# Where the split pieces of the down weights stand in the instruction order of a fused encoder layer

## The chip, the cores and the metric

The kernel runs on one core of a Trainium2 chip. A core has a matrix engine (TensorE, PE in the profile), a vector engine (VectorE, DVE), an activation engine (ScalarE, ACT), a general engine (GpSimd, POOL) and a queue engine (SyncE, SP) that issues all DMAs here. Each engine takes its instructions strictly in the order in which they stand in its queue. The metric is the device time of one launch in microseconds, median of three runs.

## The reference, cut to what matters

One encoder layer over 2048 tokens of width 1024, in float32: a normalised input projection, two groups of attention heads, an output projection with a residual, and a feed-forward block of inner width 4096. The change lies in the last one and in what leads to it:

```python
x = x + jnp.concatenate([o_mla, o_diff], axis=-1) @ w_out[layer]

h = _rmsnorm(x, mlp_norm_w[layer])
x = x + jnp.square(jax.nn.relu(h @ w_up[layer])) @ w_down[layer]
```

## The kernel before, in words

**Precision and products.** Each float32 operand is held as two float16 parts, `h` (high) and `l` (low), so that one product is three matmuls (lines 134 to 136). `split` makes the two parts: a copy on ACT (line 129 or, with a scale, line 130) and a subtraction on DVE (the same lines). Both halves of the feed-forward block use a seven-product scheme in place of eight block products, so weights and activations are first combined by additions on POOL and then split into seven pieces.

**Stages.** Projections and attention fill the first 1410 us. The output projection `out_proj` follows to about 1625 us, in 16 rounds `i`, one for each tile of 128 tokens. It also transposes the normalised tokens (`out_back`) and combines them in pairs (`combine_rows`). Tokens of the first column half (`c = 0`) stay in SBUF in seven tiles of the pool "L". Those of the second half (`c = 1`) are stored piece by piece to DRAM, `hcD`, 28 stores, and read back as `hT[1, i]`, fourteen tiles of the pool "W", 56 loads.

**Up steps.** 32 steps `n` follow, one for each pair of weight columns `p` and token half `c`. A step (`up_step`) has seven products named X1, Z5, X6, Y2, X7, Z3, X4 after their PSUM bank and number, each of 12 matmuls. X1 and X6, X7, X4 add up in the same bank, so each of them must wait until the last result has been read: X1 is copied by line 1300, Z5 by 1306, X6 by 1309 (ACT); Y2, X7 and Z3 are added by 1312, 1316 and 1321 (DVE). Line 1300 writes the tile `ca` of the pool "X4". X4 of a step is issued after X1 of the next one (`tail`). Then `up_rest` combines the results (POOL, 1350 to 1359), splits them (ACT 1346, DVE 1347) and stores them to DRAM as `uD`.

**Down steps.** Eight groups `g` of two weight pairs; in each, four double steps `i`, each for two token tiles. A double step (`down_steps`) runs the same seven names over both tiles, 14 products of six matmuls. X1, Z5 and X6 are copied out by `keep` (ACT, line 1453, into the pool "N2"); Y2, X7, Z3 and X4 are added into float32 sums by `add` (DVE, line 1457, and for three of the four names POOL, line 1459, which frees the "N2" tile).

**The pieces of the down weights.** `down_weights(g)` is a generator of 14 pieces: seven results for each of the two weight pairs, in the order in which the products of the next group use them. A piece is at most one addition on POOL (1400, 1402, 1404, 1406) and one `split` (line 130 on ACT and DVE). Its scale comes from `down_max` (maxima on DVE, 1220), `down_front` and `down_scale` (through 1376). Small pieces of work such as these are queued in `behind_products`; `tick(n)` takes the next `n` of them, so the ticks say where in the program they stand.

**What sets the order.** The matmuls are chained by hand (`ordered`). All else is placed by a list scheduler at build time: it puts on each engine what its timing model says is ready, and it gives a tile a buffer when its pool has a free one. A piece can therefore stand earlier in the engine's queue than where the program emitted it. `set_fence(ins)` remembers the last instruction of an engine, and `behind(ins)` forbids that an instruction stands ahead of it; neither adds a wait on the chip. The pools used here have 7 ("L"), 22 ("W"), 8 ("P"), 3 ("X4") and 6 ("N2") buffers.

Of the kernel before, what the change touches and what calls it, by code (L numbers as in the profile page):

```python
# [50 lines left out]
def encoder_layer(ctx: ExitStack, tc: tile.TileContext, a, out, stop=None):  # L51
# [192 lines left out]
    oD = [dram(f"oD{i}", [P, 2 * H, P]) for i in range(NT)]  # L244
    x2D = [dram(f"x2D{i}", [P, D]) for i in range(NT)]

    hcD = [dram(f"hcD{i}", [P, 7, 2, 512], F16) for i in range(4)]

    uD = [dram(f"uD{g}", [8, P, GP, 7, 2, P], F16) for g in range(NPAIR // GP)]

# [823 lines left out]
    def out_back(t):  # L1074
        y = ys.pop(t)
        if t == 0:
            for i in range(7):
                b = sb("L", [P, 2, 4, 512], F16)
                hT[0, i] = b[:, 0], b[:, 1]
        st = stage[t] = sb("P", [P, 2, 512])  # L1080
        for hf in range(2):
            pt = ps()
            for k in range(4):
                c = 4 * hf + k
                ordered(nc.tensor.transpose(pt[:, k * P : (k + 1) * P], y[:, c * P : (c + 1) * P], ident))
            for k in range(4):
                c = W_ML + 4 * hf + k
                act(st[:, hf, k * P : k * P + P], pt[:, k * P : k * P + P], AF.Copy, scale=wvec[:, c : c + 1])
        if t < 8:
            return  # L1090
        tq = t % 4

        def put(i, x):
            if t < 12:
                split(hT[0, i][0][:, tq], hT[0, i][1][:, tq], x)
            else:
                o = sb("N2", [P, 2, 512], F16)
                split(o[:, 0], o[:, 1], x)
                dma(hcD[tq][:, i].rearrange("p l c -> p (l c)"), o.rearrange("p l c -> p (l c)"))

        behind_products.append(combine_rows(stage.pop(t - 8), stage.pop(t), put))

# [2 lines left out]
    def out_proj():  # L1105
# [12 lines left out]
        for i, t in enumerate(order):  # L1118
            if i + 2 < NT:
                ot[i + 2] = out_scale(*out_load(order[i + 2]))  # L1120
            hfs = (0, 1)[i == 0 :]
            out_mid(t, 0, *mix, hfs)
            tick(2)
            nxt = list(out_front(ot.pop(i + 1))) if i + 1 < NT else [None]
            if i >= 2:
                out_back(order[i - 2])
            tick(1)
            out_mid(t, 1, *mix, hfs)
            mix = nxt[-1]
            if i == 1:  # L1130
                ml_setup()
            out_norm(t)
            tick(2)
            if i == 3:
                down_load(0, "W")
            if i == 4:
                behind_products.append(down_max(0))
            for p, j in enumerate((4, 7, 13)):
                if i == j:
                    up_load(p, "W" if p < 2 else "X4")  # L1140
                if i == j + 1:
                    behind_products.append(up_stat(p))
                if i == j + 3 and p < 2:
                    up_scale(p)
                    behind_products.append(up_weights(p))
            yield
# [69 lines left out]
    def down_max(g):  # L1216

        m = dmx[g] = small("dmx", [P, 2 * GP])
        for i, r in enumerate(rawd[g]):
            V.tensor_reduce(m[:, i : i + 1], r.rearrange("p h c -> p (h c)"), AX, ALU.max, apply_absolute_value=True)  # L1220
            yield
        if g == 0:
            rawd.pop(g)
# [52 lines left out]
    def up_step(n, c, p, hook, per):  # L1276
# [15 lines left out]

        u11, u21, u12, u22 = ca[:, 0], ca[:, 1], cb[:, 0], cb[:, 1]

        def square(x):
            act(x, x, AF.Relu)
            act(x, x, AF.Square)

        prod(X, 1, True)
        act(u11, X, AF.Copy, scale=US)  # L1300
# [2 lines left out]
        tails.clear()  # L1303
        tick(per)
        prod(Z, 5, True)
        act(u22, Z, AF.Copy, scale=US)
        tick(per)
        prod(X, 6, False)
        act(u12, X, AF.Copy, scale=US)  # L1309
        tick(per)  # L1310
        prod(Y, 2, True)
        V.scalar_tensor_tensor(u11, Y, US, u11, ALU.mult, ALU.add)
        square(u11)
        tick(per)
        prod(X, 7, False)
        V.scalar_tensor_tensor(u22, X, US, u22, ALU.mult, ALU.add)
        square(u22)
        tick(per)
        hook()
        prod(Z, 3, False)  # L1320
        V.scalar_tensor_tensor(u12, Z, US, u12, ALU.mult, ALU.add)
        V.scalar_tensor_tensor(u12, u12, 0.0, u12, ALU.max, ALU.mult)
        tick(per)

        def tail():
# [56 lines left out]

    def down_weights(g):

        t = [sb("L", [P, 2, GP, 2, 512], F16) for _ in range(3)] + [sb("W", [P, 1, GP, 2, 512], F16)]
        w = wdn[g] = [t[s // 2][:, s % 2] for s in SLOT]
        r = rawd.pop(g)
        sums = [sb("X4", [P, 2, 512]) for _ in range(GP)]

        def put(q, i, x):  # L1390
            c = dsc[g][:, q : q + 1]
            split(w[i][:, q, 0], w[i][:, q, 1], x, c)

        for j in range(7):
            for q in range(GP):
                ra, rb_ = r[2 * q : 2 * q + 2]
                b11, b12, b21, b22 = ra[:, 0], ra[:, 1], rb_[:, 0], rb_[:, 1]
                t1, t2 = sums[q][:, 0], sums[q][:, 1]
                if j == 0:
                    G.tensor_tensor(t1, b12, b11, ALU.subtract)  # L1400
                elif j == 1:
                    G.tensor_tensor(t2, b22, t1, ALU.subtract)
                elif j == 2:
                    G.tensor_tensor(b12, b22, b12, ALU.subtract)
                elif j == 4:
                    G.tensor_tensor(b21, b21, t2, ALU.subtract)
                put(q, *((0, b11), (3, t1), (4, t2), (1, b21), (5, b12), (2, b22), (6, b21))[j])
                yield

# [23 lines left out]
    TURN = ({"X": 0, "Z": 2, "Y": 4}, {"X": 6, "Z": 4, "Y": 2})  # L1433

    def down_steps(g, n, taus, hook):
        part = {}
        bk = {(t, b): bank[TURN[n % 2][b] + i] for i, t in enumerate(taus) for b in "XYZ"}
        w, lam = wdn[g], dsc[g][:, GP + 2 : GP + 3]

# [10 lines left out]
        def keep(t, name, to):  # L1450

            part[t, to] = x = sb("N2", [P, 512])
            act(x, bk[t, name], AF.Copy, scale=lam)  # L1453

        def add(t, name, to):
            x = accs[t][to]
            V.scalar_tensor_tensor(x, bk[t, name], lam, x, ALU.mult, ALU.add)  # L1457
            if (t, to) in part:
                G.tensor_tensor(x, x, part.pop((t, to)), ALU.add)  # L1459

        for name, n, first, then, to in (
            ("X", 1, True, keep, 0),
# [9 lines left out]
            for t in taus:  # L1472
                prod(t, name, n, first)
                then(t, name, to)
                tick(1)

    steps = [(p, c) for c in range(2) for p in range(4)]
    steps += [(p, c) for p in range(4, NPAIR - 2) for c in range(2)]
# [5 lines left out]
    for n, (p, c) in enumerate(steps):  # L1484
# [2 lines left out]
            drain(made[n])  # L1487
        if n == 1:
            drain(made["tokens"])
            for i in range(7):  # L1490
                b = hT[1, i] = [sb("W", [P, 4, 512], F16) for _ in range(2)]
                for l in range(2):
                    for tq in range(4):
                        dma(b[l][:, tq], hcD[tq][:, i, l])
        if n and nxt is not None:
            made[n + 1] = up_weights(nxt)
            behind_products.insert(0, made[n + 1])
# [2 lines left out]
        if n == last_step - 1:  # L1500
            down_load(0, "L")
        if n == last_step:
            made["down"] = down_weights(0)
            behind_products.append(made["down"])
            down_u(0, (0, 1), "L")

        def hook():
# [8 lines left out]
                    behind_products.append(made[nxt3, "stat"])  # L1516
            if n == 3:
                down_scale(0)

        up_step(n, c, p, hook, 4 if n in (0, last_step) else 2)  # L1520
        if nxt2 is not None and nxt2 not in scaled:
            if (nxt2, "stat") in made:
                drain(made[nxt2, "stat"])
# [99 lines left out]
```

## Time and profile before

| | |
|---|---|
| median of 3 runs | 2865.11 us (2864.14 to 2866.52) |
| profiled execution | 2862.0 us, its span 2860.2 us |
| mean granted TensorE clock | 0.987 |
| busy, share of the span | PE 94%, DVE 75%, ACT 61%, POOL 60% |
| up steps | about 1625 to 2247 us |
| down steps | about 2247 to 2857 us |

The span runs from the first instruction to the last; the 1.8 us beside it are start and end. A busy PE is not a PE at its peak. A full-speed product of 512 columns starts 0.216 us after the one before, and an idle PE shows as a larger step between two starts.

### The profile page before, as it was taken

The page shows a single profiled execution, that of the slowest core. Times are in us where ns is not written, and L with a number is a line of the kernel's source. Part 1 is how long each engine was busy: PE and PEld are TensorE (multiplying, and loading weights), DVE is VectorE, ACT ScalarE, POOL GpSimd, SP SyncE. Part 2 cuts the span into 40 slices and gives each one's busy share as a digit, 9 for nine tenths or more (in the row PEclk, how much of TensorE's full clock was granted, in tenths as well). Part 3 has the DMA queues.
Part 4 walks back from the last instruction along what each step waited for, and adds up shares of the span by engine and source line. Part 5 has one row for each costly group of instructions (what it writes and reads, how often), then busy time and mean ns, then how long its engine had stood idle before and what let it go on. Part 6 is the DMA issues. An engine that isn't in the chain of part 4 may idle for free. (4 is left out here: it accounts for less than half of the span.)

```text
span 2860.2 us, 47994 instructions
## 1 busy us (share of the span) xinstructions
PE 2686.4 (94%) x16904; PEld 1574.4 (55%) x16904; DVE 2140.0 (75%) x4292; ACT 1735.5 (61%) x3814; POOL 1715.3 (60%) x1404
## 2 busy tenths in 40 slices
PE   7999998999999999889899988999999899999999
PEld 6878885666656666556555434444444344444444
DVE  8767778999998999889868777777776655555543
ACT  6545556888888888778757656666666433333332
POOL 5434334888888888778724355444444755565544
PEclk9999999999999999999999999999999999999999
DMA  5445557998999999899844753444444643333334
GB/s 194 123 116 133 136 131 186 199 204 184 203 207 200 195 203 204 189 197 188 207 165 146 241 175 107 133 133 133 133 146 158 234 151 133 133 123 116 133 103 169
DMA packets 994514, 469.35 MB, mean 164 GB/s; under 512 B 776128, under 2 KB 943040, under 8 KB 994272
## 3 DMA queue, kind: packets, MB, share of 16 engines
q1 hardware_dynamic: 994272, 466.29, 62.7%
q8 instruction: 132, 2.16, 0.3%
q14 instruction: 110, 0.90, 0.1%
HBM read 168.39 MB, written 132.12 MB: 105 GB/s over the span
## 5 line engine op out<-in xcount | busy, mean ns | idle before, releaser
L762 ACT ACTIVATE P<-D,nm,one 128x512 f32<-128x512 f32 x768 | 587.2, 774 | 132.0 <-DVE nm L756 70.8
L735 PE MATMUL D<-W,X 128*128 128x512 f16 x2304 | 573.0, 384 | 61.6 <-ACT P L762 58.7
L819 POOL TENSOR_TENSOR L<-P,L 128x1024 f16<-128x1024 f32 x256 | 553.9, 2172 | 32.4 <-ACT L L813 21.8
L750 DVE TENSOR_REDUCE nmx<-D 128x1 f32<-128x512 f32 (+3 forms) x768 | 450.8, 619 | 38.3 <-PE D L735 32.1
L836 PE MATMUL O<-W,L 128*128 128x128 f16 x2048 | 363.0, 220 | 16.3 <-DMA L<-L 9.1
L1459 POOL TENSOR_TENSOR W<-W,N 128x512 f32<-128x512 f32 x192 | 242.6, 1273 | 222.6 <-DVE W L1457 220.0
L735 PEld LDWEIGHTS <-X 128*128 128x128 f16 x2304 | 214.2, 99 | 282.7 <-issue 94.3
L837 PE MATMUL O<-W,L 128*128 128x128 f16 x2048 | 362.8, 220 | 1.1 <-DVE W L130 1.1
L838 PE MATMUL O<-W,L 128*128 128x128 f16 x2048 | 363.0, 220 | 0.0
L1457 DVE SCALAR_TENSOR_TENSOR W<-D,dsc,W 128x512 f32<-128x512 f32 x224 | 166.3, 747 | 255.8 <-PE D L136 255.8
L134 PE MATMUL D<-W,W 128*128 128x512 f16 (+2 forms) x822 | 313.6, 382 | 24.1 <-ACT P L1309 11.4
L135 PE MATMUL D<-W,W 128*128 128x512 f16 (+2 forms) x822 | 313.3, 381 | 3.2 <-DVE W L130 3.2
L136 PE MATMUL D<-W,W 128*128 128x512 f16 (+2 forms) x822 | 312.9, 381 | 0.6 <-DVE W L130 0.5
L140 POOL TENSOR_SCALAR L<-P 128x1024 f16<-128x1024 f32 x128 | 223.1, 1743 | 138.7 <-ACT P L762 138.7
L134 PE MATMUL D<-L,W 128*128 128x512 f16 (+1 forms) x644 | 249.5, 387 | 18.0 <-ACT X L1300 12.1
L134 PE MATMUL D<-L,P 128*128 128x512 f16 x648 | 247.1, 381 | 14.5 <-ACT N L1453 14.2
L135 PE MATMUL D<-L,W 128*128 128x512 f16 (+1 forms) x644 | 247.4, 384 | 0.0
L136 PE MATMUL D<-L,W 128*128 128x512 f16 (+1 forms) x644 | 247.3, 384 | 0.0
L135 PE MATMUL D<-L,P 128*128 128x512 f16 x648 | 246.9, 381 | 0.0
L136 PE MATMUL D<-L,P 128*128 128x512 f16 x648 | 246.8, 381 | 0.0
L836 PEld LDWEIGHTS <-L 128*128 128x128 f16 x2048 | 201.2, 98 | 53.0 <-DMA L<-L 15.7
L837 PEld LDWEIGHTS <-L 128*128 128x128 f16 x2048 | 201.2, 98 | 46.2 <-issue 12.8
(421 smaller groups left out, 5729.5 us busy)
## 6 DMA issues: line engine op xcount, KB each, us to landing
P<-uD SPq DMA_DIRECT2D x124, 448.0 KB, 4.9
uD<-P SPq DMA_DIRECT2D x96, 512.0 KB, 3.2
P<-in_w_up_dram SPq DMA_DIRECT2D x34, 512.0 KB, 4.7
W<-in_w_down_dram SPq DMA_DIRECT2D x32, 512.0 KB, 4.1
X<-in_x_dram SPq DMA_DIRECT2D x17, 512.0 KB, 3.6
vD<-N SPq DMA_DIRECT2D x32, 256.0 KB, 2.6
qA<-N SPq DMA_DIRECT2D x32, 256.0 KB, 2.6
oD<-N SPq DMA_DIRECT2D x128, 64.0 KB, 2.6
```

Source lines behind the costliest of these rows:

```text
L134: mm(o, ah, bh, start=first, stop=False, skip_group_check=more),
L135: mm(o, ah, bl, start=False, stop=False, skip_group_check=more),
L136: mm(o, al, bh, start=False, stop=last, skip_group_check=more),
L140: return G.tensor_scalar(o, i, sc, 0.0, ALU.mult, ALU.add)
L735: ordered(mm(s, st, mv[:, kc], start=j == 0, stop=j == len(self.passes) - 1))
L750: ordered(V.tensor_reduce(self.nmx[:, self.n : self.n + 1], s[:, c0 * P : c1 * P], AX, ALU.max))
L762: last_exp[:] = [act(o, self.ch[c], AF.Exp, bias=self.nm, scale=self.sg, accum_out=self.sm[:, c : c + 1])]
L819: ordered(G.tensor_tensor(hl[:, 1], self.soft[d].p[hf], hl[:, 0], ALU.subtract))
L836: ordered(mm(od, hT_, v[:, 0], start=kb == 0, stop=False))
L837: ordered(mm(od, hT_, v[:, 1], start=False, stop=False))
L838: ordered(mm(od, lT_, v[:, 0], start=False, stop=kb == NT - 1))
L1459: G.tensor_tensor(x, x, part.pop((t, to)), ALU.add)
```

## The change

- `down_steps`: each `keep` and `add` sets the fence of its engine. In the double steps `i` = 2 and 3 a tick follows only the first of the two tiles' products, so 7 pieces fall in each of the two instead of all 14 in `i` = 2.
- `down_weights`: all its instructions stand behind the fences. The tile of the seventh result is taken from "W" only when it is made. For the first group the sums lie in "P" and no longer in "X4".
- `down_max`: the maxima stand behind the fence.
- In the last two up steps the copies, squares and additions set fences. The first group's pieces are queued from the hook of the last but one up step, no longer from the start of the last; the last up step takes three pieces at each tick and no longer four.
- `up_load` of pair 2 takes its raw weights from "W" and no longer from "X4".
- `hcD` is laid out by result and not by tile of tokens: 28 stores as before, each in rows of 1 KB instead of 2 KB, and 14 loads in rows of 4 KB instead of 56 in rows of 1 KB. A load now needs the stores of all four tiles. The loads are emitted in two up steps (five results at `n` = 1, two at `n` = 2).

```diff
-    hcD = [dram(f"hcD{i}", [P, 7, 2, 512], F16) for i in range(4)]
+    hcD = [dram(f"hcD{i}", [2, P, 4, 512], F16) for i in range(7)]
...
-                dma(hcD[tq][:, i].rearrange("p l c -> p (l c)"), o.rearrange("p l c -> p (l c)"))
+                dma(hcD[i][:, :, tq].rearrange("l p c -> p l c"), o)
...
-                    up_load(p, "W" if p < 2 else "X4")
+                    up_load(p, "W")
...
# down_max
-            V.tensor_reduce(m[:, i : i + 1], r..., AX, ALU.max, apply_absolute_value=True)
+            behind(V.tensor_reduce(m[:, i : i + 1], r..., AX, ALU.max, apply_absolute_value=True))
...
# up_step
+        mark = set_fence if n >= last_step - 1 else lambda *ins: None
         def square(x):
             act(x, x, AF.Relu)
-            act(x, x, AF.Square)
+            mark(act(x, x, AF.Square))
...
-        act(u22, Z, AF.Copy, scale=US)
+        mark(act(u22, Z, AF.Copy, scale=US))
...      (the same for u12 after X6, and for the additions after Y2, X7 and Z3)
# down_weights
-        t = [sb("L", ...) for _ in range(3)] + [sb("W", [P, 1, GP, 2, 512], F16)]
-        w = wdn[g] = [t[s // 2][:, s % 2] for s in SLOT]
+        t = [sb("L", ...) for _ in range(3)]
+        w = wdn[g] = [t[s // 2][:, s % 2] for s in SLOT[:6]]
-        sums = [sb("X4", [P, 2, 512]) for _ in range(GP)]
+        sums = [sb("X4" if g else "P", [P, 2, 512]) for _ in range(GP)]
         def put(q, i, x):
-            split(w[i][:, q, 0], w[i][:, q, 1], x, c)
+            behind(*split(w[i][:, q, 0], w[i][:, q, 1], x, c))
         for j in range(7):
+            if j == 6:
+                w.append(sb("W", [P, GP, 2, 512], F16))
...
-                    G.tensor_tensor(t1, b12, b11, ALU.subtract)
+                    behind(G.tensor_tensor(t1, b12, b11, ALU.subtract))
...      (the same for the other three additions)
# down_steps
-        part = {}
+        part, rare = {}, n >= 2
...
-            act(x, bk[t, name], AF.Copy, scale=lam)
+            set_fence(act(x, bk[t, name], AF.Copy, scale=lam))
...
-            V.scalar_tensor_tensor(x, bk[t, name], lam, x, ALU.mult, ALU.add)
+            set_fence(V.scalar_tensor_tensor(x, bk[t, name], lam, x, ALU.mult, ALU.add))
             if (t, to) in part:
-                G.tensor_tensor(x, x, part.pop((t, to)), ALU.add)
+                set_fence(G.tensor_tensor(x, x, part.pop((t, to)), ALU.add))
...
-                tick(1)
+                if not rare or t == taus[0]:
+                    tick(1)
# the loop over up steps
-            for i in range(7):
+        if n in (1, 2):
+            for i in ((0, 3, 4, 1, 5), (2, 6))[n - 1]:
                 b = hT[1, i] = [sb("W", [P, 4, 512], F16) for _ in range(2)]
                 for l in range(2):
-                    for tq in range(4):
-                        dma(b[l][:, tq], hcD[tq][:, i, l])
+                    dma(b[l].rearrange("p t c -> p (t c)"), hcD[i][l].rearrange("p t c -> p (t c)"))
...
         if n == last_step:
-            made["down"] = down_weights(0)
-            behind_products.append(made["down"])
             down_u(0, (0, 1), "L")
         def hook():
...
+            if n == last_step - 1:
+                made["down"] = down_weights(0)
+                behind_products.append(made["down"])
-        up_step(n, c, p, hook, 4 if n in (0, last_step) else 2)
+        up_step(n, c, p, hook, {0: 4, last_step: 3}.get(n, 2))
```

More of the change, by code (lines that the diff above doesn't have):

```diff
@@ L1219, in down_max @@
         for i, r in enumerate(rawd[g]):
-            V.tensor_reduce(m[:, i : i + 1], r.rearrange("p h c -> p (h c)"), AX, ALU.max, apply_absolute_value=True)
+            behind(V.tensor_reduce(m[:, i : i + 1], r.rearrange("p h c -> p (h c)"), AX, ALU.max, apply_absolute_value=True))
             yield
@@ L1305, in up_step @@
         prod(Z, 5, True)
-        act(u22, Z, AF.Copy, scale=US)
+        mark(act(u22, Z, AF.Copy, scale=US))
         tick(per)
         prod(X, 6, False)
-        act(u12, X, AF.Copy, scale=US)
+        mark(act(u12, X, AF.Copy, scale=US))
         tick(per)
         prod(Y, 2, True)
-        V.scalar_tensor_tensor(u11, Y, US, u11, ALU.mult, ALU.add)
+        mark(V.scalar_tensor_tensor(u11, Y, US, u11, ALU.mult, ALU.add))
         square(u11)
@@ L1315, in up_step @@
         prod(X, 7, False)
-        V.scalar_tensor_tensor(u22, X, US, u22, ALU.mult, ALU.add)
+        mark(V.scalar_tensor_tensor(u22, X, US, u22, ALU.mult, ALU.add))
         square(u22)
@@ L1321, in up_step @@
         V.scalar_tensor_tensor(u12, Z, US, u12, ALU.mult, ALU.add)
-        V.scalar_tensor_tensor(u12, u12, 0.0, u12, ALU.max, ALU.mult)
+        mark(V.scalar_tensor_tensor(u12, u12, 0.0, u12, ALU.max, ALU.mult))
         tick(per)
@@ L1383, in down_weights @@
     def down_weights(g):
-        t = [sb("L", [P, 2, GP, 2, 512], F16) for _ in range(3)] + [sb("W", [P, 1, GP, 2, 512], F16)]
-        w = wdn[g] = [t[s // 2][:, s % 2] for s in SLOT]
+        t = [sb("L", [P, 2, GP, 2, 512], F16) for _ in range(3)]
+        w = wdn[g] = [t[s // 2][:, s % 2] for s in SLOT[:6]]
         r = rawd.pop(g)
-        sums = [sb("X4", [P, 2, 512]) for _ in range(GP)]
+        sums = [sb("X4" if g else "P", [P, 2, 512]) for _ in range(GP)]
         def put(q, i, x):
             c = dsc[g][:, q : q + 1]
-            split(w[i][:, q, 0], w[i][:, q, 1], x, c)
+            behind(*split(w[i][:, q, 0], w[i][:, q, 1], x, c))
         for j in range(7):
+            if j == 6:
+                w.append(sb("W", [P, GP, 2, 512], F16))
             for q in range(GP):
@@ L1399, in down_weights @@
                 if j == 0:
-                    G.tensor_tensor(t1, b12, b11, ALU.subtract)
+                    behind(G.tensor_tensor(t1, b12, b11, ALU.subtract))
                 elif j == 1:
-                    G.tensor_tensor(t2, b22, t1, ALU.subtract)
+                    behind(G.tensor_tensor(t2, b22, t1, ALU.subtract))
                 elif j == 2:
-                    G.tensor_tensor(b12, b22, b12, ALU.subtract)
+                    behind(G.tensor_tensor(b12, b22, b12, ALU.subtract))
                 elif j == 4:
-                    G.tensor_tensor(b21, b21, t2, ALU.subtract)
+                    behind(G.tensor_tensor(b21, b21, t2, ALU.subtract))
                 put(q, *((0, b11), (3, t1), (4, t2), (1, b21), (5, b12), (2, b22), (6, b21))[j])
```

## Prediction

> **What bounds the kernel now.** I read the first page, then the waits of PE in four windows, then the timelines of single engines around the longest of these waits.
>
> ```profile
> span 2860.2 us, 47994 instructions
> PE 2686.4 (94%) x16904; PEld 1574.4 (55%) x16904; DVE 2140.0 (75%) x4292; ACT 1735.5 (61%) x3814; POOL 1715.3 (60%) x1404
> ...
> PE D L134 <- ACT X L1300: 12.1, 2, 11.3
> PE D L134 <- ACT P L1309: 1.2, 1, 1.2
> ...
> PE D L134 <- ACT P L1309: 15.0, 8, 2.8
> ...
> PE D L134 <- DVE P L1316: 5.3, 1, 5.3
> PE D L134 <- ACT N L1453: 2.6, 1, 2.6
> PE D L134 <- ACT P L1309: 0.9, 1, 0.9
> ...
> PE D L134 <- ACT N L1453: 14.2, 7, 2.4
> PE D L134 <- DVE W L1457: 3.3, 7, 0.7
> ```
>
> The matrix engine bounds the kernel. The wait rows (idle in total, times, longest) are of the windows 1625 to 1668, 1668 to 2218, 2218 to 2266 and 2266 to 2860 us. The number of matmuls doesn't change, so the change can only give back these waits, 55 us in all, or add new ones. Idle understates a stall: a full-speed product follows the last after 0.216 us but is shown as busy for 0.38, so each stall costs 0.16 us more, and after some of them PE runs at half speed for a while (below). The 15.0 us in the second window lie in steps that the change doesn't touch.
>
> **Term 1, the down groups.** This is one of the seven groups that prepare the next; the others look the same.
>
> ```profile
> 2436.45 1.33 ACT L130 ACTIVATE L<-W,dsc 128x512 f16<-128x512 f32 x2 [8.68 <-DVE dsc L1376]
> 2437.69 2.54 ACT L130 ACTIVATE L<-X,dsc 128x512 f16<-128x512 f32 x4
> 2440.14 3.77 ACT L130 ACTIVATE L<-W,dsc 128x512 f16<-128x512 f32 x6
> 2443.82 2.38 ACT L1453 ACTIVATE N<-D,dsc 128x512 f32<-128x512 f32 x4
> ...
> 2444.53 0.38 PE L134 MATMUL D<-L,P 128*128 128x512 f16 x1 [1.78 <-ACT N L1453]
> ...
> 2439.53 2.73 DVE L130 SCALAR_TENSOR_TENSOR L<-X,dsc,L 128x512 f16<-128x512 f32 x4
> ...
> 2451.97 1.21 DVE L1220 TENSOR_REDUCE dmx<-W 128x1 f32<-128x1024 f32 x1
> 2453.10 1.39 DVE L1457 SCALAR_TENSOR_TENSOR W<-D,dsc,W 128x512 f32<-128x512 f32 x2
> ...
> 2455.98 0.38 PE L134 MATMUL D<-W,P 128*128 128x512 f16 x1 [0.66 <-DVE W L1457]
> ...
> 2596.98 0.38 PE L134 MATMUL D<-L,P 128*128 128x512 f16 x1 [2.35 <-ACT N L1453]
> 2598.14 0.63 PE L135 MATMUL D<-L,P 128*128 128x512 f16 x1
> 2600.70 0.50 PE L135 MATMUL D<-L,P 128*128 128x512 f16 x1
> ```
>
> As soon as the scale is there, ACT runs twelve splits in a row (7.4 us), and the four copies that free X wait behind them: PE loses 1.78 + 0.16 us. The DVE maxima of a later group stand ahead of the additions and cost two shorter stalls. Between the stalls at 2444.53 and 2596.98 lie two groups: 152.5 us, 76.2 each. A double step has 14 x 6 = 84 matmuls; four of them with two small ones are 338 x 0.216 = 72.9 us. So a group loses 3.3 us, and seven groups 23 to 24: 17.5 us of idle, 14 x 0.16, twice about 1.7 us of half speed after a stall of 2.35 (from the row at 2598.14 to that at 2600.70 six steps take 2.56 us, 0.43 each), and about 1 us of gaps too short for the list.
>
> After the change no split stands ahead of the `keep` or `add` before it, and one piece comes to two products, 2.59 us. In the copy phase ACT has two copies of 0.60 and a split of 0.64 there (rows: 2.38 and 2.54 for four): 1.8 us, no queue. In the adding phase DVE has two additions of 0.70 and a subtraction of 0.68 (1.39 for two, 2.73 for four): 2.1 us. The tied maxima go to the start of the second double step, when no additions are due; the scale is taken at the same point as before. The last piece comes with the last product of the group, but it feeds the seventh product of the next one, 12 products or 15.5 us later; pieces are made in the order of use. The raw tiles come free some 18 us later, so the four loads of a later group move to the first double step, 18 us before their maxima. "W" still suffices: 16 sums, 4 raw tiles, 2 seventh pieces are its 22.
>
> ```profile
> 2448.79 3.26 DVE L130 SCALAR_TENSOR_TENSOR W<-W,dsc,W 128x512 f16<-128x512 f32 x2
> ...
> 2443.00 5.59 POOL L1406 TENSOR_TENSOR W<-W,X 128x512 f32<-128x512 f32 x2 [5.38 <-DVE L L130]
> 2451.46 1.71 POOL L1404 TENSOR_TENSOR W<-W,W 128x512 f32<-128x512 f32 x1
> 2453.98 1.27 POOL L1459 TENSOR_TENSOR W<-W,N 128x512 f32<-128x512 f32 x1 [0.80 <-DVE W L1457]
> ```
>
> What hides the pieces is slack: a copy or addition has three products (3.9 us) before its bank is written again. If POOL runs beside it, a subtraction takes up to 1.63 us (3.26 for two) and the pair of products 3.0 instead of 2.59. Over three pairs that is a lag of 1.3 us, still inside 3.9 less the 0.7 of the addition. I take 22.5 of the 24 us, with ends 10 (a lag comes back as 1 us of stall in each of 14 double steps) and 24.
>
> [...]
>
> [...]
>
> **Term 2, the step after the output projection.**
>
> ```profile
> 1660.66 0.58 PE L134 MATMUL D<-L,W 128*128 128x512 f16 x1 [11.27 <-ACT X L1300]
> ...
> 1659.13 0.68 DVE L1347 TENSOR_TENSOR N<-X,N 128x512 f16<-128x512 f32 x1
> ...
> 1660.03 0.57 ACT L1300 ACTIVATE X<-D 128x512 f32<-128x512 f32 x1
> ...
> 1644.00:1662.00 18.00, 6.74 (x29) 2.85 (x28) 17.97 (x18) 11.58 (x16) 11.22 (x8) 0.72 0.91 288
> ```
>
> Line 1300 of step 1 started 0.2 us after line 1347 had read the last of step 0's `ca`. The pool "X4" has three buffers, and the raw weights of pair 2 held two. With "W" for these, `ca` has a buffer at once and the stall of 11.4 us goes, and with it the half speed after it, about 2 us by the 1.7 above: 13.4 together. What is late next: the window row (us; busy of PE, PEld, DVE, ACT, POOL; clock; DMA share and GB/s) shows DVE full and the DMA at 0.91 in this stretch. Up to there a stall covered them. Moreover, the loads of `hcD` now wait for the last stores and come after 1640 us, where before they began at 1606 (row below).
>
> ```profile
> L116 SPq DMA_DIRECT2D W<-hcD x56: 319/430/2193, 1606.1 to 1655.8; - x56
> W<-x2D SPq DMA_DIRECT2D x16, 512.0 KB, 9.0
> 2244.82 8.28 SPq L116 DMA_DIRECT2D W<-x2D  x8
> ```
>
> SP gains: 56 issues of 0.43 us (24 us of its queue) become 14. The bytes stay, 14 tiles of 512 KB; eight loads of this form and size were let go in 8.28 us, about 1.2 us each when back to back, so 14 take some 17 us: 1640 to 1665 us, with uD stores and raw weights between them. They are first needed in step 4: step 1 began three products before the stall (1649 - 7.8), and three steps of 18.1 later it is 1696. Stores of `uD` behind them may land 5 us later and hold "P" buffers. I take 4 us of new stall (ends 0 and 11), and 1 us back from line 1309 in step 0, which stood behind splits of the tokens: 10.4 us. The 28 stores have twice the rows, 256 KB each as before; at 28 spread over 70 us I cost them at nothing, bounded by the 4 us.
>
> **Term 3, the end of the up steps.**
>
> ```profile
> 2221.25 1.27 POOL L1400 TENSOR_TENSOR X<-L 128x512 f32<-128x512 f32 x1
> 2232.88 2.13 POOL L1400 TENSOR_TENSOR X<-L 128x512 f32<-128x512 f32 x1 [1.88 <-issue]
> ...
> 2232.67 1.21 DVE L1347 TENSOR_TENSOR P<-X,P 128x1024 f16<-128x1024 f32 x1
> 2240.50 1.75 DVE L130 SCALAR_TENSOR_TENSOR L<-X,dsc,L 128x512 f16<-128x512 f32 x1
> 2242.17 0.68 DVE L1316 SCALAR_TENSOR_TENSOR P<-D,P 128x512 f32<-128x512 f32 x1
> ...
> 2242.90 0.59 PE L134 MATMUL D<-W,W 128*128 128x512 f16 x1 [5.26 <-DVE P L1316]
> ...
> 2260.69 0.69 ACT L1453 ACTIVATE N<-D,dsc 128x512 f32<-128x512 f32 x1 [1.82 <-POOL W L1459]
> ```
>
> The first sums waited for "X4" buffers until 2221 and 2233, so the pieces crowded the last 20 us, each subtraction at up to 1.75 us. Here 5.26 + 2.63 + 0.9 us of idle, three times 0.16 and about 1.5 us of half speed make 10.8. After the change the sums have "P" buffers, and the POOL additions, which no fence of these steps holds, can run 15 us earlier. But the splits that ran ahead in step 30 are tied too: 14 subtractions of 0.68 (9.5 us), those of `up_rest` (3 x 1.21 + 0.68) and four additions of 0.68 are 16.5 us of DVE in a step of 84 x 0.216 = 18.1. It fits with little to spare; three pieces between two products can hold line 1316 up to 2 us too long, and the "N2" wait at 2260.69 can partly stay. The two "L" tiles of the first activations are now taken after the three of the pieces, some microseconds later than now and some 30 before their use: nothing. I take 3 us of new stalls (ends 0 and 11): 7.8 us gained.
>
> **The sum.** 22.5 + 10.4 + 7.8 = 40.7 us from the profiled execution of 2862.0 us, which stands 3.1 us under the median of 2865.1. Prediction 2824 us.
>
> **Rivals.**
> A. Part of the stalls come back. For: POOL in double steps 2 and 3 has 12 additions of line 1459 and 8 of the pieces, 20 x 1.27 = 25.4 us; its row of 5.59 for two beside DVE's splits shows that these can hold it up, and if each of the 14 does so for its whole 0.68, 9.5 more make 34.9 of 36.3 us. DVE is full in step 1. Against: the blocks rarely meet in full. If 1.5 us stay in each group and terms 2 and 3 give half: 13.5 + 9.1 = 23 us, 2842.
> B. The fences only forbid earlier places; the scheduler puts the pieces later, and they crowd at the end of the group. Then the first products of the next one wait as now: term 1 goes, terms 2 and 3 stay at 18, 2847; if the same holds in step 31, 2855. Against: a ready piece was always taken at once.
> C. No change: term 1 by B, and DVE and DMA in step 1 hand back the 10 us of term 2: within 6 us of 2865.
> D. Slower: POOL becomes the bound of double steps 2 and 3. At a mean of 2.3 us per addition, as POOL's row of 2.13 or 5.59 for two suggest, 20 take 46 us for 36.3, 10 over; through "N2" the copies and so PE wait for it. Seven times 10, less 41, is 29 us slower, 2894. It decides from (36.3 + 41/7)/20 = 2.1 us on. Against: those rows lie beside unbroken DVE work, which the change breaks up; line 1459 alone shows 1.27.
>
> **How the numbers follow.** Forecast 0.62 (2806 to 2835), A and B together 0.23 (2835 to 2856), C 0.06, D 0.09. A measurement here can tell about 0.2%, 5.7 us. Faster 0.85, same 0.06, slower 0.09. Lower end: all three terms in full, 24 + 14.4 + 10.8 = 49, and a further 8 of the 15 us of line 1309 by a luckier order: 2808, put at 2807. Upper end: A and most of B, 2850. The likeliest case alone spans 2810 to 2835.
>
> **What would show it.** Term 1: splits of line 130 single between copies of line 1453, no PE wait on line 1453 in double step 2, groups of 73 us. Term 2: no PE wait on line 1300; loads of `hcD` after 1640 us. Term 3: line 1400 near 2200, the wait on line 1316 under 2 us. Wrong would be: PE waits on line 1457 or on "N2" in both double steps, POOL without gaps there, or a first matmul of step 4 that waits for `hcD`.

## The result and the profile after

The changed kernel takes 2832.81 us (median of four runs; 2828.2 to 2836.23) against 2865.12 us (2864.14 to 2866.52) before: a ratio of 0.9882 with a 95% interval of 0.9867 to 0.9896, 32.3 us less. The forecast was 2824. The profiled execution of the changed kernel took 2831.03 us. Lines below 1300 keep their numbers; 1300 is now 1302, 1309 is 1311, 1316 is 1318, 1346 and 1347 are 1348 and 1349, 1453 is 1458, 1457 is 1462 and 1459 is 1464.

The first page, its two lines on the span and the engines:

```profile
span 2829.2 us, 47941 instructions
...
PE 2684.3 (95%) x16904; PEld 1574.7 (56%) x16904; DVE 2169.4 (77%) x4292; ACT 1738.0 (61%) x3814; POOL 1713.2 (61%) x1404
```

The busy time of PE is the same as before to 2 us, so the gain is time in which PE no longer stands. The waits of PE after the change (idle in total, times, longest), in the windows 1625 to 1668, 1668 to 1900, 2218 to 2266 and 2266 to 2829 us:

```profile
PE D L134 <- ACT X L1302: 0.8, 1, 0.8
...
PE D L134 <- ACT P L1311: 8.1, 6, 2.3
PE D L136 <- DVE W L130: 7.3, 5, 4.2
PE D L134 <- ACT W L130: 3.1, 2, 2.9
...
PE D L134 <- ACT N L1458: 2.0, 1, 2.0
...
PE D L134 <- ACT N L1458: 0.4, 1, 0.4
```

The kernel before had, in the second of these windows:

```profile
PE D L134 <- ACT P L1309: 12.8, 6, 2.8
PE D L136 <- DVE W L130: 0.5, 1, 0.5
```

The last window, seven down groups, has lost its 17.5 us of idle but for 0.4. In the third the 5.3 us on the addition is gone. In the first the 12.1 us on line 1300 is down to 0.8. But in the second, in steps whose matrix work the change doesn't touch, 10.4 us of waits for splits of line 130 stand where 0.5 us stood.

A stall costs more than its idle, as the prediction worked out (0.16 us more each, from 0.38 and 0.216 us a product, and half speed after some), so I also summed by how much each matmul starts later than 0.216 us after the start before it. Figures called lost below are such sums over the records of a trace, in us:

| window | before | after |
|---|---|---|
| 1620 to 1668, step 1 | 17.0 | 3.8 |
| 1668 to 1900 | 14.6 | 25.0 |
| 1900 to 2215 | 2.8 | 3.2 |
| 2215 to 2266 | 10.8 | 2.5 |
| 2266 to the end | 24.4 | 0.6 |

That is 34.5 us less, and the profiled executions differ by 31.0. The rest lies in the attention stage, which the change does not touch: matmul number 10,349, at its end, starts at 1412.2 us in the trace of before and at 1416.0 in that of after, and between 1411.5 and 1420.1 in all traces of this case. Some differences below are therefore also given as one trace of each kernel shows them from that matmul to the last.

How a down group looks now, ACT and then DVE, in order of time, from the changed kernel:

```profile
2426.66 0.69 ACT L1458 ACTIVATE N<-D,dsc 128x512 f32<-128x512 f32 x1 [11.18 <-PE D L136]
2427.25 0.71 ACT L130 ACTIVATE L<-W,dsc 128x512 f16<-128x512 f32 x1
2427.97 0.69 ACT L1458 ACTIVATE N<-D,dsc 128x512 f32<-128x512 f32 x1
...
2435.05 0.74 DVE L130 SCALAR_TENSOR_TENSOR L<-X,dsc,L 128x512 f16<-128x512 f32 x1
2435.71 0.74 DVE L1462 SCALAR_TENSOR_TENSOR W<-D,dsc,W 128x512 f32<-128x512 f32 x1
...
2442.84 1.66 DVE L130 SCALAR_TENSOR_TENSOR L<-W,dsc,L 128x512 f16<-128x512 f32 x1
```

One split stands between two copies, where twelve stood in a row, and one subtraction between two additions; that of 2442.84, with two additions of POOL beside it (line 1464, 2442.69 to 2445.62 us), takes 1.66 us, and still no product waits for an addition.

### The profile page after: what moved, and what is told of

Read it like the earlier page. It is cut to its first block, busy times and chain, and to the rows that moved or that the text cites. A ratio compares the mean times of both kernels' runs of the same rounds, so it can differ in the third digit from the quotient of the medians.

```text
span 2829.2 us, 47941 instructions
## 1 busy us (share of the span) xinstructions
PE 2684.3 (95%) x16904; PEld 1574.7 (56%) x16904; DVE 2169.4 (77%) x4292; ACT 1738.0 (61%) x3814; POOL 1713.2 (61%) x1404
## 4 chain that ended last, share of the span: by engine, by line
PE 36%; DVE 7%; ACT 2%; POOL 2%; DMA 2%; issue 2%; POOLq 0%; SPq 0%; ACTq 0%; DVEq 0%
PE D L134 10%; PE D L136 10%; PE D L135 10%; DVE W L130 2%; DVE P L1349 1%; PE O L134 1%; PE O L136 1%; PE O L135 1%; DMA uD<-P 1%; DVE N L1171 1%; ACT P L1348 1%; DMA P<-in_w_up_dram 1%; POOL P L1352 0%; POOL P L1353 0%; DVE P L1324 0%
## 5 line engine op out<-in xcount | busy, mean ns | idle before, releaser
L1464 POOL TENSOR_TENSOR W<-W,N 128x512 f32<-128x512 f32 x192 | 262.4, 1381 | 235.9 <-DVE W L1462 224.8
L1458 ACT ACTIVATE N<-D,dsc 128x512 f32<-128x512 f32 x160 | 109.8, 687 | 209.4 <-PE D L136 204.4
L836 PEld LDWEIGHTS <-L 128*128 128x128 f16 x2048 | 201.4, 98 | 51.6 <-DMA L<-L 14.1
```

What stands on the lines that cost most here:

```text
L836: ordered(mm(od, hT_, v[:, 0], start=kb == 0, stop=False))
L1464: set_fence(G.tensor_tensor(x, x, part.pop((t, to)), ALU.add))
```

## Where the time came back

The reading goes backwards from the first long new stall, with PE, then ACT and POOL of the changed kernel:

```profile
1691.45 0.39 PE L134 MATMUL D<-L,W 128*128 128x512 f16 x1 [2.85 <-ACT W L130]
...
1693.90 0.63 PE L136 MATMUL D<-L,W 128*128 128x512 f16 x1
...
1685.25 1.06 ACT L1348 ACTIVATE P<-X 128x1024 f16<-128x1024 f32 x1 [4.52 <-DMA uD<-P]
1690.68 0.72 ACT L130 ACTIVATE W<-N,rb_b 128x512 f16<-128x512 f32 x1 [1.04 <-POOL N L1193]
...
1687.71 1.26 POOL L1361 TENSOR_TENSOR X<-X,P 128x512 f32<-128x512 f32 x1 [12.40 <-DVE P L1349]
1688.94 1.71 POOL L1193 TENSOR_TENSOR N<-P 128x512 f32<-128x512 f32 x1
```

PE waits for a split of the next pair's weights; that split waits for POOL's sum on line 1193; the sum stands in POOL's order behind line 1361, for which POOL idles 12.40 us; line 1361 needs the last read of a hidden block, lines 1348 and 1349; and line 1348 waits 4.52 us until a store of `uD` lets go of a "P" buffer. After the stall PE runs at half speed (the row of 0.63 us; such products start 0.43 us apart, and the granted clock is 0.50 from 1693.4 to 1696.6 us): with it and two short waits for the next splits, 6.5 us are lost from 1688 to 1699 us.

Why is the store late? SP of the changed kernel, and then the answers for the tile `hcD` and, from 1650 to 1692 us, for the tile `uD` (in the `hcD` row: ns of an issue, shortest, median and longest, then the us at which the first and the last start):

```profile
1654.37 3.60 SPq L116 DMA_DIRECT2D W<-hcD  x7
1658.06 0.38 SPq L116 DMA_DIRECT2D uD<-P  x1
...
1671.93 3.29 SPq L116 DMA_DIRECT2D W<-hcD  x4
1676.42 2.78 SPq L116 DMA_DIRECT2D uD<-P  x2
...
L116 SPq DMA_DIRECT2D W<-hcD x14: 333/441/1238, 1637.4 to 1674.3; - x14
...
DMA to landing us min/median/max: 4.0/7.6/12.1
```

Each load reads the rows of all four tiles of tokens, so it can't be let go before the last tile's store. After three single ones they come in bursts, seven (3.5 MB) and then four, with `uD` stores right behind. A store lands up to 12.1 us after its issue, that of 1658.06; the first of the two from 1676.42, behind the four loads, lands at 1685.2, and then line 1348 starts. Over the whole kernel the median to landing is 3.2:

```profile
uD<-P SPq DMA_DIRECT2D x96, 512.0 KB, 3.2
```

These rows show the order and the times, not that the loads ahead make a store late; loads_by_tile and last_loads_later below test that.

A second place, 1754 to 1768 us, loses 8.4 us in the same trace, 4.2 of them in one wait for a split: a raw tile of `w_up` arrives late, and the square of line 1168, which waits for it, stands ahead of two splits on ACT:

```profile
1753.14 1.06 ACT L1168 ACTIVATE N<-P 128x1024 bf16<-128x1024 f32 x1 [3.07 <-DMA P<-in_w_up_dram]
```

## The experiments

The kernels ran in three sets of four, each set on one chip beside the kernel before. The median of before was 2866.7 us in the first set (up to after_pair2_in_x4), 2865.81 in the second (no_fence_in_groups, all_ticks_in_third, old_layout_of_tokens, squares_behind_splits) and 2866.55 in the third.

### Each part alone

The theory is that three parts act in separate windows and that their gains add up, with the second reduced by new stalls; the rival is that they need each other.

**groups_alone**: of the change, only the fences in `down_steps`, `behind` in `down_max` and `down_weights`, the seventh piece's own "W" tile and the ticks over two double steps.

```diff
-            split(w[i][:, q, 0], w[i][:, q, 1], x, c)
+            behind(*split(w[i][:, q, 0], w[i][:, q, 1], x, c))
...
-            act(x, bk[t, name], AF.Copy, scale=lam)
+            set_fence(act(x, bk[t, name], AF.Copy, scale=lam))
...
-                tick(1)
+                if not rare or t == taus[0]:
+                    tick(1)
```

> The kernel before with the edits of the down groups alone: fences in the double steps, pieces and maxima behind them, a tick after only the first tile in the last two double steps; tokens, pool of pair 2 and the first group as before. Theory (the term of the groups is worth what the changed kernel's trace shows there, 24 us, and stands by itself): 23 to 25 us faster than before, groups of 73 us. Rival (the groups' gain is partly due to the earlier stages, which then set other places for the scheduler): under 18 us.

Measured 2839.7 us (2837.77 to 2843.17), 0.9908 [0.9887, 0.9929]: 27.0 us less. Waits of PE in the windows from 1625, from 2215 and from 2266 us:

```profile
PE D L134 <- ACT X L1300: 12.1, 2, 11.3
...
PE D L134 <- DVE P L1316: 5.3, 1, 5.3
...
PE D L134 <- ACT N L1455: 1.1, 2, 0.7
```

The 17.5 us of the groups are down to 1.1, and the long stalls of the other two terms stand as before. In the trace the groups lose 1.4 us in place of 24.4. The "N2" wait of 2.6 us at the first double step is gone too, which the prediction had put into term 3. Term 1 is right.

**end_alone**: the fences of the last two up steps, `down_weights(0)` from the last but one step, its sums in "P", the ticks of that step; nothing in `down_steps`.

```diff
+        mark = set_fence if n >= last_step - 1 else lambda *ins: None
...
-        sums = [sb("X4", [P, 2, 512]) for _ in range(GP)]
+        sums = [sb("X4" if g else "P", [P, 2, 512]) for _ in range(GP)]
...
+            if n == last_step - 1:
+                made["down"] = down_weights(0)
+                behind_products.append(made["down"])
```

> The kernel before with the edits of the first group alone: fences in the last two up steps, the pieces from the last but one step's hook, three ticks, sums in P. Theory: 7 to 9 us faster, the wait on the second DVE addition of the last up step under 2 us. Rival (that wait went because DVE was freed of the maxima and POOL of the next group's additions, which the fences of the down steps hold back): under 4 us, with the wait on the copy of the first double step still above 2 us.

Measured 2862.14 us (2856.46 to 2870.15), 0.9986 [0.9974, 0.9999]: 4.6 us less, of which the trace puts only 1.1 in this window (lost 9.7 for 10.8). The wait on the addition, line 1316 of before, is gone; in its stead one of the first group's copies comes 6.3 us late (the kernel's line 1457 in the window from 2215):

```profile
PE D L134 <- ACT N L1457: 6.3, 1, 6.3
```

The rows of DVE, POOL and ACT ahead of that copy:

```profile
2253.32 2.33 DVE L1220 TENSOR_REDUCE dmx<-W 128x1 f32<-128x1024 f32 x2
...
2255.71 1.26 POOL L1404 TENSOR_TENSOR X<-W 128x512 f32<-128x512 f32 x1
...
2258.22 0.69 ACT L1457 ACTIVATE N<-D,dsc 128x512 f32<-128x512 f32 x1 [1.82 <-POOL W L1463]
```

Without fences in the down steps, the maxima and sums of the following group (lines 1220 and 1404) were put ahead of the additions of the first group, and the copy waits for an "N2" buffer, which a POOL addition of that group, line 1463, lets go. Alone, the fences of the up steps gain 1.1 us in this window and those of the down steps 2.6 (lost 8.2 in groups_alone); together they gain 6.6 to 8.3 (groups_and_end below, and the whole change). So this window needs both.

**tokens_alone**: the layout of `hcD`, its 14 loads over two steps, and pair 2's raw weights in "W".

```diff
-    hcD = [dram(f"hcD{i}", [P, 7, 2, 512], F16) for i in range(4)]
+    hcD = [dram(f"hcD{i}", [2, P, 4, 512], F16) for i in range(7)]
...
-                    up_load(p, "W" if p < 2 else "X4")
+                    up_load(p, "W")
...
-                    for tq in range(4):
-                        dma(b[l][:, tq], hcD[tq][:, i, l])
+                    dma(b[l].rearrange("p t c -> p (t c)"), hcD[i][l].rearrange("p t c -> p (t c)"))
```

> The kernel before with the new layout of the tokens in DRAM, 14 loads split over two up steps, and the raw weights of pair 2 in W. Theory (the 11 us wait goes, but the stores of the up steps land behind the later loads and the steps up to 1785 us give most of it back): 0 to 4 us faster, no wait of PE on the first copy of step 1, new waits on the splits of the up weights between 1685 and 1770 us. Rival (the net gain of this part is what was forecast, 10 us, and the loss has its origin in the fences or in the attention stage): 9 to 12 us faster.

Measured 2862.32 us (2858.5 to 2865.66), 0.9988 [0.9979, 0.9998]: 4.4 us less. Step 1 loses 3.8 us in place of 17.0, but the window from 1668 loses 25.6 in place of 14.6. Its waits:

```profile
PE D L136 <- DVE W L130: 7.3, 5, 4.2
PE D L134 <- ACT P L1309: 6.2, 4, 2.3
PE D L134 <- ACT W L130: 3.0, 2, 1.8
```

The waits for splits are those of the changed kernel, so the token part makes them by itself.

### The buffer of pair 2

**after_pair2_in_x4**: the changed kernel with pair 2's raw weights in "X4" again.

```diff
-                    up_load(p, "W")
+                    up_load(p, "W" if p < 2 else "X4")
```

> The changed kernel with the raw weights of pair 2 in X4 again, all else as changed. Theory (the wait of step 1 comes from that pool): the wait of PE on the first copy of step 1 is back at 9 to 12 us; but it gives the loads and stores time, so that the later waits up to 1770 us shrink, and the time is only 0 to 6 us above that of the changed kernel. Rival (the wait came from somewhere else): no such wait, and the time of the changed kernel.

Measured 2833.77 us (2832.65 to 2835.45), 0.989 [0.9872, 0.9907]: the same as the changed kernel to 1 us. Waits from 1625 and from 1668 us:

```profile
PE D L134 <- ACT X L1302: 11.8, 2, 11.0
...
PE D L134 <- ACT P L1311: 11.4, 5, 2.8
PE D L136 <- DVE W L130: 0.5, 1, 0.5
```

The stall of step 1 is back, and the waits for splits are gone but for 0.5 us, as in the kernel before. With the 14 late loads, the long stall covers most of what otherwise comes up behind it: counted from matmul 10,349, this trace is only 3.3 us longer than the changed kernel's.

### The fences and the ticks of the groups

**no_fence_in_groups**: the changed kernel, with `behind` only for the first group's pieces and for no maxima.

```diff
+        tie = behind if g == 0 else lambda *ins: None
...
-            behind(*split(w[i][:, q, 0], w[i][:, q, 1], x, c))
+            tie(*split(w[i][:, q, 0], w[i][:, q, 1], x, c))
```

> The changed kernel with the pieces and the maxima of the later seven groups free of fences again; the ticks stay spread over two double steps. Theory (the fences end the waits of the groups, the spread alone doesn't, since a ready piece is taken at once): the seven waits of PE on the copies of the third double step are back, 18 to 24 us slower than the changed kernel, near 2855 us. Rival (the later emission alone keeps the pieces back): within 4 us of the changed kernel.

Measured 2858.64 us (2851.02 to 2866.11), 0.9975 [0.9962, 0.9988], 25.8 us slower than with the fences. From 2215 and from 2266 us (the copies are line 1459 here):

```profile
PE D L134 <- ACT N L1459: 6.3, 1, 6.3
...
PE D L134 <- ACT N L1459: 15.2, 8, 2.4
```

The groups lose 26.6 us in place of 0.6, as the theory has it. The stall at the first double step is the one of end_alone (lost 9.1 in place of 2.5 from 2215 to 2266 us); the expectation had left it out.

**all_ticks_in_third**: a piece behind each product of the third double step, so that a group's pieces come in one double step instead of two.

```diff
-                if not rare or t == taus[0]:
-                    tick(1)
+                tick(1)
```

> The changed kernel with a tick after every product again, so that all 14 pieces are tied in the third double step and none in the fourth. Theory (what hides the pieces is slack of one piece to two products; two pieces to two products are 3.4 to 4 us of DVE in 2.59): the additions of the third double step lag and PE waits on line 1462 or on the copies, 1 to 3 us in each of seven groups, 7 to 20 us slower than the changed kernel. Rival (the fence is enough, engines have room): within 3 us.

Measured 2831.29 us (2830.93 to 2837.46), 0.9883 [0.9868, 0.9898]: no difference from the changed kernel. All waits of PE from 2266 us:

```profile
PE O L134 <- ACT N L1458: 0.8, 4, 0.2
```

The theory fell. The additions do lag: in the group at 2440 us they start 1.68 us apart (at 2440.56, 2442.24, 2443.92 and 2445.60) with a subtraction of 1.09 us between them, where a product comes each 1.30 us. But over one double step the slack behind a copy or addition, estimated at three products in term 1, takes up that lag but for 0.2 us at a time. So the fences carry the whole of term 1 and the slower pace nothing that shows.

### The layout of the tokens

**old_layout_of_tokens**: the changed kernel with the 56 loads and four arrays of before; pair 2 stays in "W", and the loads are still asked for in steps 1 and 2.

```diff
-    hcD = [dram(f"hcD{i}", [2, P, 4, 512], F16) for i in range(7)]
+    hcD = [dram(f"hcD{i}", [P, 7, 2, 512], F16) for i in range(4)]
...
-                    dma(b[l].rearrange("p t c -> p (t c)"), hcD[i][l].rearrange("p t c -> p (t c)"))
+                    for tq in range(4):
+                        dma(b[l][:, tq], hcD[tq][:, i, l])
```

> The changed kernel with the tokens stored by tile as before and 56 loads, still emitted in two up steps; pair 2 stays in W. Theory (the late loads hold up the stores of the up steps, and those hold P buffers): the loads of three of the four tiles go before 1640 us, the waits on splits between 1685 and 1700 us (6.5 us) go, those from 1750 on may stay; 3 to 8 us faster than the changed kernel. Rival (without the wait of step 1 the vector and general engines are simply full there, whatever the transfers do): the same waits, within 3 us of the changed kernel.

Measured **2819.58 us (2818.15 to 2826.09), 0.9843 [0.9826, 0.986]**: 13.2 us less than the changed kernel, the fastest of these kernels. Its loads of `hcD`, and its waits from 1668 us:

```profile
L116 SPq DMA_DIRECT2D W<-hcD x56: 319/424/1998, 1608.2 to 1671.7; - x56
...
PE D L134 <- ACT P L1311: 10.2, 6, 2.5
PE D L136 <- DVE W L130: 2.1, 1, 2.1
```

The loads begin 29 us earlier, as each tile's stores are done. The stall on line 1302 is down to 0.9 us, and the window behind it adds nothing: 15.1 us are lost from 1668 to 1900, as before the change (14.6).

**loads_by_tile**: the layout and the stores of the change, but a load for each tile of tokens. It tells the loads' late start from the shape of the stores.

```diff
-                    dma(b[l].rearrange("p t c -> p (t c)"), hcD[i][l].rearrange("p t c -> p (t c)"))
+                    for tq in range(4):
+                        dma(b[l][:, tq], hcD[i][l, :, tq])
```

> The changed kernel with its new layout and its stores (rows of 1 KB), but the tokens read back tile by tile in 56 loads, as before the change. Old layout with such loads gave 2819.6 us, the changed kernel 2832.8. Theory (what costs is that a load covers all four tiles and so can't start before the last tile is stored): 2818 to 2824 us, loads from about 1606 us on, no waits on splits between 1685 and 1770 us. Rival 1 (the stores' smaller rows, or the grouping of the tiles in DRAM tensors, cost the 13 us): within 3 us of the changed kernel. Rival 2 (the order of the queue of SP is what differs): between the two.

Measured 2820.91 us (2819.16 to 2827.24), 0.9849 [0.9831, 0.9868]: like the old layout. The row of its loads, the line on the landing of `uD` from 1650 to 1692 us, and POOL:

```profile
L116 SPq DMA_DIRECT2D W<-hcD x56: 319/427/1848, 1608.3 to 1672.0; - x56
...
DMA to landing us min/median/max: 2.8/5.3/6.9
...
1679.65 1.27 POOL L1361 TENSOR_TENSOR X<-X,P 128x512 f32<-128x512 f32 x1 [6.77 <-DVE P L1349]
```

The stores of `uD` land within 6.9 us in place of 12.1, and POOL's line 1361 runs 8 us earlier, 2 of which come from the attention stage. So the cost is that one load covers four tiles; the rows of the stores cost nothing that shows. This run makes the loads earlier and smaller at once, so it doesn't tell the later start from the size of a transfer.

**last_loads_later**: the changed kernel with the last four loads asked for in step 3 instead of step 2.

```diff
-        if n in (1, 2):
+        if n in (1, 3):
...
-            for i in ((0, 3, 4, 1, 5), (2, 6))[n - 1]:
+            for i in ((0, 3, 4, 1, 5), (2, 6))[n // 2]:
```

> The changed kernel with the last four of its 14 token loads emitted one up step later (step 3 and not step 2). Theory (these four loads, let go between 1672 and 1674 us, hold up two stores of uD that landed at 1685 and 1687, which holds a buffer of P, an ACT split, POOL and the next pair's splits): the wait of 4.5 us on that store goes, and the stall of 6.5 us at 1688 to 1697 us goes or comes 18 us later; 0 to 6 us faster than the changed kernel. Rival (the first ten loads alone do the damage): the stall stays at 1688 us.

Measured 2825.29 us (2823.51 to 2826.79), 0.9862 [0.9845, 0.988]: 7.5 us less than the changed kernel. POOL's line 1361 runs at 1677.26 us (matmul 10,349 starts 4.5 us earlier in this trace, so some 6 of the 10 us are the edit's), and 1.2 us of waits for subtractions of splits are left from 1668 to 1900:

```profile
PE D L134 <- ACT P L1311: 12.9, 7, 3.7
PE D L136 <- DVE W L130: 1.2, 2, 0.7
```

A store that stands behind the first burst still lands late there (up to 11.5 us after its issue in this stretch), but the four loads, 2 MB, no longer stand ahead of the one that line 1348 waits for: its wait in this stretch is 1.2 us in place of 4.5. In exchange PE waits longer on line 1311, 12.9 us in place of 8.1. The window loses 20.5 us in place of 25.0, so the edit gives back a third to a half of what the layout costs.

**groups_and_end**: the changed kernel without its token part (old layout, loads in step 1, pair 2 in "X4").

```diff
-    hcD = [dram(f"hcD{i}", [2, P, 4, 512], F16) for i in range(7)]
+    hcD = [dram(f"hcD{i}", [P, 7, 2, 512], F16) for i in range(4)]
...
-                    up_load(p, "W")
+                    up_load(p, "W" if p < 2 else "X4")
```

> The changed kernel without the whole part on the tokens and pair 2: groups and end of the up steps alone. Theory (this part removes 11 us plus half speed and its layout gives 10 back): 2831 to 2836 us, no different from the changed kernel by more than 3 us; the end of the up steps gains what neither part gave alone, 8 us between 2215 and 2266 us. Rival (the part is worth its 10 us of forecast in company): 2842 us or more.

Measured 2831.91 us (2829.65 to 2836.8), 0.9886 [0.9868, 0.9904]: no different from the whole change. From 2215 to 2266 us it loses 4.2 us in place of 10.8, a gain of 6.6 where 8 was expected. Waits from 1625 and from 1668 us:

```profile
PE D L134 <- ACT X L1302: 12.1, 2, 11.3
...
PE D L134 <- ACT P L1311: 11.2, 6, 2.8
```

Four kernels with the same groups and end now stand side by side, each as the difference of its median to that of the kernel before in the same set. In brackets stands the same difference from the traces, from matmul 10,349 to the last, without the attention stage:

| | pair 2 in "X4" | pair 2 in "W" |
|---|---|---|
| tiles loaded one by one | -34.6 us (-30.5) | -46.2 us (-44.9) |
| four tiles in one load | -32.9 us (-31.4) | -32.3 us (-34.8) |

Freeing "X4" is worth 11.6 us (14.4 by the traces) with the old loads and next to nothing (3.3) with the new ones; the new loads cost nothing clear of noise (1.7, or a gain of 0.9) while the stall covers them and 13.9 us (10.2) once it is gone. The kernel of the first cell also asks for all its loads in step 1, the others in two steps.

### Two trials with the order of the splits

**squares_behind_splits**: in the changed kernel, the squares of line 1168 and their sums are kept behind the splits made so far on the same engine, to shorten the second place above.

```diff
-            act(sq, r.rearrange("p h (k f) -> p (h k) f", f=P), AF.Square)
+            after_splits(act(sq, r.rearrange("p h (k f) -> p (h k) f", f=P), AF.Square))
...
-        split(w[0][:, :, 0], w[0][:, :, 1], ra, c)
+        keep_order(*split(w[0][:, :, 0], w[0][:, :, 1], ra, c))
```

> The changed kernel with the squares and sums of the raw up weights tied behind the splits of the pair that is made at that time. Theory (in step 5 to 6 the ACT queue holds a square ahead of three splits, and it waits for a load that landed at 1753): the waits on splits at 1754 to 1768 us, 8.4 us, go, and 5 to 9 us are gained. Rival (the splits are late for their additions on POOL): the waits stay, and PE waits longer for the sums of squares at the end of the steps, 0 to 5 us slower.

Measured 2847.34 us (2845.65 to 2850.28), 0.9935 [0.992, 0.995], 14.5 us slower than the changed kernel. The waits for splits are gone, but the sums of squares are now late, and with them the small products on line 1187 that need them; a second wait there is 10.3 us long:

```profile
PE O L1187 <- DVE N L1182: 12.3, 1, 12.3
```

The tie was too coarse, and it doesn't settle how much of the second place is due to the late raw tile and how much to the order on ACT. Neither the two kernels with loads by tile nor last_loads_later have a wait of over 2 us between 1754 and 1768 us, so this place too goes with the late loads.

**old_layout_copy_first**: the old layout, with the copy of line 1311 ahead of the hidden block's reads and two ticks moved behind it, to win the waits that stood there before the change too.

```diff
+        early = 2 if per == 2 else 0
-        tick(per)
+        tick(per - early)
...
+            if i in (0, 2) and u12_copy:
+                tc.add_manual_dep(hi.ins, u12_copy[0].ins.name, NOSYNC, reason="order")
```

> The changed kernel with the tokens stored as before (2819.6 us) and, besides, the copy after X6 put ahead of the second and third split of the results on ACT. Theory (PE's remaining waits on that copy, about 14 us between 1675 and 1810 us, come from those splits standing ahead of it while they wait for P buffers): the waits go, 5 to 12 us faster than 2819.6. Rival (what is held back then makes the next pair's splits late): the waits move to the splits, 0 to 10 us slower than 2819.6.

Measured 2826.23 us (2819.79 to 2831.86), 0.9863 [0.9842, 0.9884], 6.7 us slower than the old layout alone; the two intervals overlap, but the trace from matmul 10,349 on is longer by as much, 7.1 us. From 1668 us the waits on the copy (line 1312) fall to 1.4 us, and others take their place:

```profile
PE D L136 <- DVE W L130: 7.6, 8, 2.9
PE D L134 <- ACT P L1312: 1.4, 2, 0.7
```

So in these steps the order chose who was late; that no other order does better isn't shown.

## Why the prediction was right and wrong

**Term 1, right.** 22.5 us were taken of 24; the trace loses 0.6 us where it lost 24.4, and the part alone gave 27.0 [20.4, 32.4]. The fences do it, as costed. The pace over two double steps, with which the lag was bounded, was not needed. The price of the subtraction beside POOL, up to 1.63 us, was right (1.66 above) and hidden.

**Term 3, right in size, incomplete in reason.** 7.8 us were forecast and 8.3 measured (10.8 less 2.5), and the partial "N2" wait stayed at 2.0 us. The first sums start at 2206.83 us, where "near 2200" was said. But the term was worked out from the up steps alone, and alone they give 1.1 us there: that the next group's sums and maxima would jump ahead at the first double step was not in it. Forecast together with the down steps' fences, the size came out; that it did so without this reason is in part luck.

**Term 2, the step that failed.** That the 11.3 us of line 1300 go was right. The failing step is "I take 4 us of new stall (ends 0 and 11)": the window from 1668 us loses 10.4 us more than before, near the upper end, and by the table the new loads cost 10.2 us (traces) to 13.9 (times). The net of the term was 1 us alone and 4 in company by the traces instead of 10.4 (4.4 us and none by the times). In the windows of the trace term 2 falls 7.6 us short, the other two are 1.8 us above their forecast, and the rest of the 8.8 us between 2824 and 2832.8 is of the size by which executions differ in the attention stage. Its parts were named in it, the later start, the stores of `uD` behind the loads, the "P" buffers, but priced by how long they would be late (5 us) and not by who stands behind the buffers: line 1348, then line 1361 on POOL, then the next pair's sums and splits, then 2.85 us of PE at a stretch and the half speed after it. Also wrong was when the loads would be done: 1665 us was reckoned from eight loads let go without a pause, and the last went at 1674.3. The saving of 42 issues on SP bought nothing: loads_by_tile issues all 56 and takes 11.9 us less. The first matmul of step 4 doesn't wait for `hcD`.

**The total.** Terms 1 and 3 carry 30 of the 41 us and came out, so the time lies 9 us from the forecast although most of term 2 was lost.

**The rivals.** Part of the stalls did come back, as rival A has it, but not where it put most of them: the 1.5 us in each down group through POOL aren't there, and the loss lies in the up steps after the tokens, for which A named only that DVE is full. The pieces weren't put late (B). POOL didn't become the bound: D needed 2.1 us per addition, and those of line 1464 took 1.38 us in the mean. That each subtraction holds POOL up for its whole 0.68 us, the estimate behind A's 34.9 us, no run shows: those additions took 1.26 to 1.73 us, in the mean 0.11 more than line 1459 before.

**What stays open.** How the 8.4 us from 1754 to 1768 us divide between the late raw tile and the order on ACT; whether the new loads cost by their later start alone or also by their size; and the rest of the 15 us on line 1311, which was there before the change.

## What to carry to other kernels

One transfer that takes from several producers starts when the last is done (here the first of the 14 loads at 1637.4 us, and the first of 56 at 1608.3 in loads_by_tile); price its delay by the chain behind the buffers that queue up with it, not by the issues it saves. Where a list scheduler takes each ready piece at once, a fence that only forbids early places can remove stalls at no cost that shows, but all stages that share the engines need it, or the wait moves to the next. Before counting on a removed stall, look for what it covered: try the other edits of the change with the stall left in.

## What the runs showed of the hardware

A store of 512 KB that lands in 3.2 us in the median took 12.1 us behind seven loads of 512 KB issued just before it on the same queue. Half speed of PE followed a stall of 2.85 us (products of 0.63 us from 1693.90 us, granted clock 0.50 from 1693.4 to 1696.6). The length of the stall alone doesn't tell: in the kernel before, the one of 2.35 us at 2596.98 was followed by a granted clock of 0.50 from 2597.5 to 2600.9 us, and the one of 2.35 us at 2673.92 by a clock of 1.00.
